# A hybrid decoder layer on Trainium2: TensorE in written order through the mixer, the recurrence woven with projection pieces, and the modulation sums taken by rows

## The chip, the cores and the metric

The kernel runs on one core of a Trainium2 chip. The metric is the device time of one execution in microseconds (us). The engines are named as the profile names them: PE is TensorE (matmuls; PEld its weight loads), DVE is VectorE, ACT is ScalarE, POOL is GpSimd, SP is SyncE, which issues most loads. Each engine carries out its own instruction list in order; semaphores tie the lists together.

## The reference, cut to what matters

One layer over 2048 tokens of width 1024, float32, batch 1. The part that the change touches is the mixer:

```python
cond = silu(c)
mod = cond @ ada_w + ada_b              # six vectors of 1024: shift, scale, gate, twice
h = rms_norm(x, mix_norm_g) * (1 + scale_m) + shift_m
q_a, k_a, v_a, q_h, f_h, i_h, g_h = split(h @ w_in + b_in)
attn = rms_norm(sliding_window_gqa_with_sinks(q_a, k_a, v_a, sinks))    # window 128, 8 heads of 64
rec  = hgrn2(silu(q_h), lb + (1 - lb) * sigmoid(f_h), i_h)              # 4 heads of 128
#      f_t = forget gate; S_t = diag(f_t) S_{t-1} + (1 - f_t) i_t^T ; o_t = S_t^T q_t
rec  = rms_norm(rec) * silu(g_h)                                        # output gate
x = x + gate_m * (concat(attn, rec) @ w_out)
```

Behind it stand a second norm with its own modulation, a gated MLP with a causal convolution, and a final norm. These are not touched.

## The kernel before, in words

Every float32 product is made of three matmuls on parts rounded to a high and a low piece (`mm3`: high by high, high by low, low by high). A projection of 128 columns over 512 tokens is 24 matmuls of 128x512 into one bank of PSUM. Its weights arrive as a raw tile, ACT rounds the high piece, and DVE or POOL subtracts to get the low one (`split`), a projection or two ahead of use (`weights`, in the order of the list `units`).

The mixer runs from about 88 to 930 us, as a loop over four groups `g` of 512 tokens. In a group the projections are named by what they give: `hq`, `hf` (query and forget gate of a recurrent head), `i` (two halves of 192 matmuls of 128x256 each), `k`, `q` (tiles `ps_q`, weights `w_qp`), `v`, and `hg` (output gate of a head; tile `ps_hg`). The recurrence is worked in two pairs of heads, (0,1) and (2,3). For a pair:

- The preparation, on DVE with rounding on ACT and POOL: products `raw0` to `raw2` of query and key, running products `tot` of the forget gate, and in-place scalings of the query `a_q` and the key `K` by `tot`.
- Five levels of widths 4, 8, 16, 32, 64. A level group (`lv`) is four matmuls of one head; in between DVE scales `a_q` and `K` for the next level (`scaled`) and copies the result under a mask into `AT` (ACT does so for 32 and 64). After them three sums per head (`lv_d`, `lv` from `ph`, `pl`, `p` by `ones_r`), with four masked copies of DVE behind them, and a transpose of `K` (`ktp`).
- `hg_state`: the state update (`U`, `mid`) and the output `ho`.

Level groups, sums and `ktp` share two PSUM banks (tag `hg`); projections have three (tag `mm`). A scheduling layer orders each engine's list by the dependences that it sees and program order as priority, except where `pin` holds an engine to the order written. Before the change only ACT (`S`) is pinned, and only from place to place; PE's order is the scheduler's.

The modulation vectors of later layers are made piece by piece beside this (`after`, six places in a group): each piece is a 512 KB load of 128 columns of `ada_w` on SP's queue, then on DVE one product 128x1024 and sums of 512, 256 and 128 columns (tiles `ada`, `part`). There are 24 of them. The attention of a group is 16 units of score, softmax and value work (tiles `sc`, `comb`, `st`, `pT`, `att_o`), with the four output gates (`hg_out`: a projection, four transposes `otp`, and one DVE product into `a_g`) written behind it.

Of the kernel before, what the change touches and what calls it, by code (L numbers as in the profile page):

```python
# [8 lines left out]
F32 = mybir.dt.float32  # L9
# [9 lines left out]
P = 128  # L19
# [34 lines left out]
def kernel(ctx, tc, x, c, ada_w, ada_b, mix_norm_g, w_in, b_in, attn_sinks, attn_out_g,  # L54
# [152 lines left out]
    def mod_part(t, raw, to):  # L207

        SY.dma_start(out=raw, in_=ada_v[:, :, t * P:(t + 1) * P])
        V.tensor_tensor(out=raw, in0=raw, in1=cond.unsqueeze(2).broadcast_to([P, KT, P]), op=ALU.mult)  # L210
        for n in (4, 2):
            V.tensor_tensor(out=raw[:, 0:n, :], in0=raw[:, 0:n, :], in1=raw[:, n:2 * n, :], op=ALU.add)
        V.tensor_tensor(out=to[:, t % 4, :], in0=raw[:, 0, :], in1=raw[:, 1, :], op=ALU.add)

# [15 lines left out]
    with ExitStack() as mx:  # L230
# [103 lines left out]
        for g in range(NG):  # L334
# [6 lines left out]
            add(("i", 0), load_wi, 0)  # L341
            add(("i", 1), load_wi, 1)
# [4 lines left out]
            add(("k", 0), load_w, 512)  # L347
            add(("qp", 0), load_wq, 0)
            add(("qp", 1), load_wq, 1)
            add(("v", 0), load_w, 640)  # L350
            for h in range(4):
                add(("hg", h), load_w, 2304 + h * P)
# [223 lines left out]
        defer = list(range(16, 40))  # L576

        part = []

        def mod_cols():  # L580
            if part:
                mod_cols_of(*part.pop())
# [6 lines left out]
        for g in range(NG):  # L589
            hhi, hlo = hh  # L590

            def after():

                if defer:
                    t = defer.pop(0)
                    if t % 4 == 0:
                        mod_cols()
                        part.append((t, mt2.tile([P, 4, P], F32, tag="part", bufs=1, name=f"part_{t}")))
                    mod_part(t, mt2.tile([P, KT, P], F32, tag="ada", bufs=1, name=f"ada_{t}"), part[-1][1])

# [6 lines left out]
            def proj_i():  # L607
                i_tok = mt.tile([P, BPG, 512], F32, tag="i_tok", bufs=1, name=f"itok_{g}")
                for pp in range(2):
                    ws = weights(g, "i", pp)  # L610
                    for bp in range(2):
                        ps = bank(f"ps_i{g}_{pp}_{bp}", "mm").rearrange("p (a b) -> p a b", a=2)
                        for bb in range(2):
                            b = 2 * bp + bb
# [9 lines left out]
            def proj_attn():  # L624
# [37 lines left out]
                for b in range(BPG):  # L662
                    TE.transpose(ps[:, b * P:(b + 1) * P], vT[:, b * P:(b + 1) * P], ident)
# [921 lines left out]
```

## Time and profile before

| | us |
|---|---|
| median of three runs | 2443.85 (2443.26 to 2449.54) |
| the profiled execution, whole | 2448.34 |
| its span in the profile | 2446.3 |
| of it, the mixer's recurrence stretches (four) | 579.30 |
| of it, the mixer's attention stretches (four) | 263.10 |
| granted clock, mean | 0.975 |

The four recurrence stretches are 88 to 210.3, 274 to 426, 489 to 640 and 707 to 861 us of the span: from a group's first projections to the end of the second pair. The four attention stretches are what lies between them and up to 930. The rest of the span, before 88 and behind 930, is set-up and the MLP. The granted clock is the mean share of TensorE's full clock; a stretch at half of it reads 0.50.

### The profile page before, as it was taken

The page shows a single profiled execution, that of the slowest core. Times are in us where ns is not written, and L with a number is a line of the kernel's source. Part 1 is how long each engine was busy: PE and PEld are TensorE (multiplying, and loading weights), DVE is VectorE, ACT ScalarE, POOL GpSimd, SP SyncE. Part 2 cuts the span into 40 slices and gives each one's busy share as a digit, 9 for nine tenths or more (in the row PEclk, how much of TensorE's full clock was granted, in tenths as well). Part 3 has the DMA queues.
Part 4 walks back from the last instruction along what each step waited for, and adds up shares of the span by engine and source line. Part 5 has one row for each costly group of instructions (what it writes and reads, how often), then busy time and mean ns, then how long its engine had stood idle before and what let it go on. Part 6 is the DMA issues. An engine that isn't in the chain of part 4 may idle for free. (4 is left out here: it accounts for less than half of the span.)

```text
span 2446.3 us, 31473 instructions
## 1 busy us (share of the span) xinstructions
PE 2294.8 (94%) x11521; PEld 1904.1 (78%) x11521; DVE 1912.5 (78%) x2737; ACT 966.7 (40%) x1658; POOL 931.7 (38%) x776
## 2 busy tenths in 40 slices
PE   5889898998999899999999999999999989998997
PEld 4877787887788787887888888778888768786775
DVE  8888768788867877378888888878878688777666
ACT  3336523723552363455333333433333343233322
POOL 6222212213122222032756666478888721110101
PEclk8999999999999999999999999999999989999999
DMA  8342323323231238475434433554555488887543
GB/s 216 91 121 91 91 69 105 95 70 112 79 95 53 86 113 267 157 248 155 146 97 144 151 117 114 191 176 156 163 153 166 138 267 248 215 209 239 182 171 124
DMA packets 335445, 359.74 MB, mean 147 GB/s; under 512 B 12405, under 2 KB 279371, under 8 KB 335291
## 3 DMA queue, kind: packets, MB, share of 16 engines
q1 hardware_dynamic: 320315, 301.36, 39.3%
q0 software_dynamic: 14976, 56.37, 8.5%
q8 instruction: 91, 1.49, 0.2%
q14 instruction: 63, 0.52, 0.1%
HBM read 250.19 MB, written 107.49 MB: 146 GB/s over the span
## 5 line engine op out<-in xcount | busy, mean ns | idle before, releaser
L46 DVE SCALAR_TENSOR_TENSOR cc<-ub,cols,cc 128x1024 f32<-128x1024 f32 x88 | 153.2, 1741 | 15.5 <-ACT cc L46 13.3
L46 PE MATMUL lv<-a_q,K 128*128 128x128 f32 (+2 forms) x768 | 80.5, 265 | 42.7 <-DVE K L46 38.2
L46 ACT ACTIVATE Th<-da 128x896 fp32r<-128x896 f32 x88 | 81.8, 945 | 92.6 <-PE ps_d L46 88.2
L46 PEld LDWEIGHTS lv<-a_q,K 128*128 128x128 f32 (+2 forms) x768 | 72.2, 177 | 55.6 <-DVE K L46 28.8
L46 POOL DMA_DIRECT2D x_d<-o x32 | 27.2, 858 | 218.6 <-DVE o L46 218.6
L46 DVE TENSOR_TENSOR o<-ps_d,u 128x512 f32<-128x512 f32 x72 | 49.5, 687 | 71.6 <-ACT u L46 34.8
L46 DVE TENSOR_TENSOR Tl<-da,Th 128x896 fp32r<-128x896 f32 x88 | 94.5, 1099 | 12.8 <-ACT Th L46 12.8
L46 POOL TENSOR_TENSOR s<-wu_0r,s 128x512 f32<-128x512 f32 x44 | 59.2, 1347 | 107.2 <-DVE ws_0l L46 14.6
L46 DVE TENSOR_TENSOR cc<-cc,v 128x1024 f32<-128x1024 f32 x44 | 64.2, 1459 | 43.5 <-ACT cc L46 43.4
L46 POOL MEMSET AT<- 128x512 f32 x16 | 8.5, 533 | 234.8 <-PE ho L46 211.8
L46 POOL TENSOR_TENSOR s<-wu_1r 128x512 f32<-128x512 f32 x44 | 70.0, 1590 | 70.7 <-DVE t_T4l L46 16.2
L46 POOL TENSOR_TENSOR wu_1r<-wu_0r,wu_1r 128x512 f32<-128x512 f32 x44 | 93.3, 2121 | 3.1
L46 ACT ACTIVATE cc<-cc 128x1024 f32<-128x1024 f32 x44 | 46.7, 1061 | 120.8 <-DVE cc L46 120.8
L46 POOL TENSOR_SCALAR rv_d<-ssd 128x1 f32<-128x1 f32 x16 | 14.8, 925 | 181.6 <-ACT dx L46 181.6
L46 POOL TENSOR_TENSOR pl<-raw,ph 128x512 fp32r<-128x512 f32 x32 | 44.3, 1388 | 99.3 <-ACT ph L46 83.6
L46 POOL TENSOR_TENSOR s<-s,wu_0r 128x512 f32<-128x512 f32 x44 | 73.6, 1672 | 0.0
L46 DVE TENSOR_TENSOR v<-ps_u,v 128x512 f32<-128x512 f32 x88 | 60.4, 686 | 15.2 <-PE ps_u L46 11.9
L46 DVE COPY_PREDICATED AT<-lev,lv 128x512 f32<-128x512 uint32 (+1 forms) x96 | 70.1, 731 | 2.4 <-PE lv L46 1.1
L46 ACT ACTIVATE cc<-ub,cols 128x1024 f32<-128x1024 f32 x44 | 54.6, 1240 | 25.9 <-DVE ub L46 25.9
L46 DVE TENSOR_TENSOR ada<-ada,cond 128x1024 f32<-128x1024 f32 (+1 forms) x37 | 52.3, 1414 | 14.3 <-DMA ada<-in_ada_w_dram 14.3
L46 DVE TENSOR_TENSOR a_q<-a_q,tot 128x256 f32<-128x256 f32 x96 | 52.1, 543 | 12.4 <-PE lv L46 11.1
L46 DVE TENSOR_TENSOR ada<-ada 128x512 f32<-128x512 f32 (+3 forms) x82 | 61.2, 747 | 0.9
(2114 smaller groups left out, 8562.9 us busy)
## 6 DMA issues: line engine op xcount, KB each, us to landing
da<-act_d SPq DMA_DIRECT2D x88, 448.0 KB, 8.0
wu_0r<-in_w_up_dram SPq DMA_DIRECT2D x44, 512.0 KB, 4.6
wu_1r<-in_w_up_dram SPq DMA_DIRECT2D x44, 512.0 KB, 4.3
act_d<-cc POOLq DMA_DIRECT2D x42, 512.0 KB, 4.1
ada<-in_ada_w_dram SPq DMA_DIRECT2D x40, 512.0 KB, 6.0
x_d<-o POOLq DMA_DIRECT2D x32, 512.0 KB, 7.9
act_d<-sm POOLq DMA_DIRECT2D x21, 768.0 KB, 4.2
x<-in_x_dram SPq DMA_DIRECT2D x26, 512.0 KB, 5.6
```

The lines of the kernel that those rows point to most:

```text
L46: ins = fn(*args, **kwargs)
```

## The change

It does four things.

1. PE is pinned with ACT to written order from a group's first projection to the end of its second pair. Projections become generators that yield after each six matmuls (`steps`; `steps_i` after each twelve), and `weave` takes one such piece behind each level group, each sum and each transpose of a pair.
2. The pieces: the second half of `i` and the next `hq` go into the first pair's levels, the next `hf` into its state; `q` 2 and 3 and the output gates of heads 0 and 1 into the second pair's levels, `v` into its state. `k` moves ahead of the first pair. The weights' list follows.
3. The preparation of a head becomes a function of its own (`hg_prep`) and stands behind that head's `hf`, with other projections between it and the pair's first level.
4. The modulation sums go by rows: 48 steps, each a 256 KB load of 2 KB rows and one DVE product-and-sum 128x512, one step ahead in its load; one step before and one behind the second pair's levels, ten in each attention.

```diff
-    def mod_part(t, raw, to):
-        SY.dma_start(out=raw, in_=ada_v[:, :, t * P:(t + 1) * P])
-        V.tensor_tensor(out=raw, in0=raw, in1=cond.unsqueeze(2).broadcast_to([P, KT, P]), op=ALU.mult)
...
+        def load_mod():
...
+                raw = mt2.tile([P, 4 * P], F32, tag="ada", bufs=2, name=f"ada_{n}_{k}")
+                SY.dma_start(out=raw, in_=ada_v[:, k, 16 * P + n * 4 * P:16 * P + (n + 1) * 4 * P])
+        def mod_step():
...
+            if k == 0:
+                V.tensor_scalar(out=acc_, in0=raw, scalar1=cond[:, 0:1], scalar2=None, op0=ALU.mult)
+            else:
+                V.scalar_tensor_tensor(out=acc_, in0=raw, scalar=cond[:, k:k + 1], in1=acc_, op0=ALU.mult, op1=ALU.add)
...
+            def steps(w, name, fn):
+
+                w, ps = w(), bank(name, "mm")
+                for k in range(KT):
+                    mm3(ps, w[0][:, k, :], w[1][:, k, :], hhi[:, k, :], hlo[:, k, :], k == 0, k == KT - 1)
+                    if k % 2 and k < KT - 1:
+                        yield
+                fn(ps)
+                yield
...
+            def weave(gen, *fill):
+
+                rest = (i for one in fill for i in one)
+                next(rest, None)
+                for _ in gen:
+                    next(rest, None)
+                for _ in rest:
+                    pass
...
                     values(u)
+                    for _ in range(2 if u % 4 == 3 else 1):
+                        mod_step()
...
-                for h in range(2):
-                    proj_h(hg_q, h, "hq")
-                    proj_h(hg_f, h, "hf")
-            weights(g, "i", 0, ahead=1)
-            pin(True, S)
-            hg_scores((0, 1))
-            i_tok = proj_i()
-            hg_state((0, 1))
...
+                run(steps_h(hg_q, 0, "hq"), steps_h(hg_f, 0, "hf"), steps_h(hg_q, 1, "hq"))
+                hg_prep(0)
+                run(steps_h(hg_f, 1, "hf"))
+            hg_prep(1)
+            run(steps_i(0), steps(lambda: weights(g, "k", 0), f"ps_k{g}", take_k))
+            q2 = [] if g == 0 else [steps_h(hg_q, 2, "hq")]
+            weave(hg_scores((0, 1)), steps_i(1), *q2)
+            weave(hg_state((0, 1)), steps_h(hg_f, 2, "hf"))
+            hg_prep(2)
+            mod_step()
+            run(steps_h(hg_q, 3, "hq"), steps_h(hg_f, 3, "hf"))
+            hg_prep(3)
+            run(steps_q(0), steps_q(1))
+            weave(hg_scores((2, 3)), steps_q(2), steps_q(3), steps_h(hg_out, 0, "hg"), steps_h(hg_out, 1, "hg"))
+            mod_step()
+            weave(hg_state((2, 3)), steps(lambda: weights(g, "v", 0), f"ps_v{g}", take_v))
+            pin(False, S, TE)
+            v_tok = turn_v()
```

Three places show what this does to the engines' lists. All are of group 1 and its second pair; in the names the first number is the group, the second the head, a third the level, and the last a running number of the buffer.

On DVE, before, while head 3 is prepared (`ada_26` is a modulation piece, `kl` the key's low piece, `w1_qp` weights of `q`):

```order
L46 TENSOR_TENSOR ada_26_3707<-ada_26_3707,cond_157 128x1024
L46 SCALAR_TENSOR_TENSOR kl0_705<-ps_k1_3713,cols_137,kd0_703 64x512
L46 TENSOR_TENSOR ada_26_3707<-ada_26_3707 128x512
L46 SCALAR_TENSOR_TENSOR kl1_706<-ps_k1_3713,cols_137,kd1_704 64x512
L46 TENSOR_TENSOR ada_26_3707<-ada_26_3707 128x256
L46 TENSOR_TENSOR part_24_3353<-ada_26_3707 128x128
L46 TENSOR_TENSOR w1_qp_1_1l_3417<-w1_qp_1_0r_3418,w1_qp_1_1h_3416 128x512
L46 TENSOR_TENSOR w1_qp_1_1l_3417<-w1_qp_1_1r_3425,w1_qp_1_1h_3416 128x512
L46 TENSOR_TENSOR raw1_1_3_3460<-a_q1_3_3342,K_1_3_3406 128x256
L46 TENSOR_TENSOR raw2_1_2_3468<-a_q1_2_3258,K_1_2_3303 128x512
L46 TENSOR_TENSOR a_q1_3_3342<-a_q1_3_3342,f_1_3_3403 128x256
L46 TENSOR_TENSOR K_1_3_3406<-K_1_3_3406,f_1_3_3403 128x256
```

and DVE there now:

```order
L46 TENSOR_TENSOR w1_qp_1_0l_3422<-w1_qp_1_0r_3425,w1_qp_1_0h_3421 128x512
L46 TENSOR_TENSOR w1_qp_1_1l_3424<-w1_qp_1_0r_3425,w1_qp_1_1h_3423 128x512
L46 TENSOR_TENSOR w1_qp_1_0l_3422<-w1_qp_1_1r_3432,w1_qp_1_0h_3421 128x512
L46 TENSOR_TENSOR w1_qp_1_1l_3424<-w1_qp_1_1r_3432,w1_qp_1_1h_3423 128x512
L46 TENSOR_SCALAR f_1_3_3464<-f_1_3_3464,omc_614,lbc_612 128x512
L46 TENSOR_SCALAR K_1_3_3467<-f_1_3_3464 128x512
L46 TENSOR_TENSOR tot_1_3_1_3487<-f_1_3_3464 128x256
L46 TENSOR_TENSOR raw0_1_3_3476<-a_q1_3_3416,K_1_3_3467 128x512
L46 TENSOR_TENSOR tot_1_3_2_3495<-tot_1_3_1_3487 128x128
L46 TENSOR_TENSOR a_q1_3_3416<-a_q1_3_3416,f_1_3_3464 128x512
L46 TENSOR_TENSOR tot_1_3_4_3601<-tot_1_3_2_3495 128x64
L46 TENSOR_TENSOR raw1_1_3_3481<-a_q1_3_3416,K_1_3_3467 128x256
```

The modulation piece and the key's pieces have left the preparation; what stands in it now is the weights of `q`, ahead of it, and the head's own work.

On PE, before, where the second pair's levels begin (`lv_1_2_4` is group 1, head 2, level 4):

```order
L46 MATMUL ps_q1_1_3785<-hlo_1_2521,w1_qp_0_1h_3362 128x512
L46 MATMUL lv_1_2_4_3488<-a_q1_2_3258,K_1_2_3303 128x128 x4
L46 MATMUL lv_1_3_4_3498<-a_q1_3_3342,K_1_3_3406 128x128 x4
L46 MATMUL ps_q1_1_3785<-hhi_1_2520,w1_qp_0_1l_3363 128x512
L46 MATMUL ps_q1_2_3822<-hhi_1_2520,w1_qp_1_0h_3414 128x512
L46 MATMUL ps_q1_2_3822<-hlo_1_2521,w1_qp_1_0h_3414 128x512
L46 MATMUL ps_q1_2_3822<-hhi_1_2520,w1_qp_1_0l_3415 128x512
L46 MATMUL lv_1_2_8_3508<-a_q1_2_3258,K_1_2_3303 128x128 x4
L46 MATMUL ps_q1_2_3822<-hhi_1_2520,w1_qp_1_0h_3414 128x512
L46 MATMUL lv_1_3_8_3518<-a_q1_3_3342,K_1_3_3406 128x128 x4
L46 MATMUL ps_q1_2_3822<-hlo_1_2521,w1_qp_1_0h_3414 128x512
L46 MATMUL ps_q1_2_3822<-hhi_1_2520,w1_qp_1_0l_3415 128x512
```

and PE there now:

```order
L46 MATMUL ps_q1_2_3571<-hhi_1_2522,w1_qp_1_0l_3422 128x512
L46 MATMUL lv_1_2_4_3578<-a_q1_2_3207,K_1_2_3322 128x128 x4
L46 MATMUL ps_q1_2_3571<-hhi_1_2522,w1_qp_1_0h_3421 128x512
L46 MATMUL ps_q1_2_3571<-hlo_1_2523,w1_qp_1_0h_3421 128x512
L46 MATMUL ps_q1_2_3571<-hhi_1_2522,w1_qp_1_0l_3422 128x512
L46 MATMUL ps_q1_2_3571<-hhi_1_2522,w1_qp_1_0h_3421 128x512
L46 MATMUL ps_q1_2_3571<-hlo_1_2523,w1_qp_1_0h_3421 128x512
L46 MATMUL ps_q1_2_3571<-hhi_1_2522,w1_qp_1_0l_3422 128x512
L46 MATMUL lv_1_3_4_3594<-a_q1_3_3416,K_1_3_3467 128x128 x4
L46 MATMUL ps_q1_2_3571<-hhi_1_2522,w1_qp_1_0h_3421 128x512
```

The first level group used to stand in the middle of `ps_q1_1`, with one to three projection matmuls behind each of the next; it now comes behind `ps_q1_0`, `ps_q1_1` and six matmuls of `ps_q1_2`, and six follow each level group.

On DVE, before, from the first level group on (`a_q` and `K` by `tot_1_2_2` are the scaling of head 2 that its level 8 needs):

```order
L46 TENSOR_TENSOR a_q1_2_3258<-a_q1_2_3258,tot_1_2_2_3482 128x64x4
L46 TENSOR_TENSOR K_1_2_3303<-K_1_2_3303,tot_1_2_2_3482 128x64x4
L46 COPY_PREDICATED AT_1_2_3432<-lev4_680,lv_1_2_4_3488 128x512
L46 TENSOR_TENSOR a_q1_3_3342<-a_q1_3_3342,tot_1_3_2_3486 128x64x4
L46 TENSOR_TENSOR K_1_3_3406<-K_1_3_3406,tot_1_3_2_3486 128x64x4
L46 COPY_PREDICATED AT_1_3_3433<-lev4_680,lv_1_3_4_3498 128x512
L46 TENSOR_TENSOR a_q1_2_3258<-a_q1_2_3258,tot_1_2_4_3495 128x32x8
L46 TENSOR_TENSOR K_1_2_3303<-K_1_2_3303,tot_1_2_4_3495 128x32x8
L46 COPY_PREDICATED AT_1_2_3432<-lev8_685,lv_1_2_8_3508 128x512
L46 TENSOR_TENSOR a_q1_3_3342<-a_q1_3_3342,tot_1_3_4_3505 128x32x8
L46 TENSOR_TENSOR K_1_3_3406<-K_1_3_3406,tot_1_3_4_3505 128x32x8
L46 COPY_PREDICATED AT_1_3_3433<-lev8_685,lv_1_3_8_3518 128x512
```

and DVE there now:

```order
L46 TENSOR_TENSOR a_q1_2_3207<-a_q1_2_3207,tot_1_2_2_3368 128x64x4
L46 TENSOR_TENSOR K_1_2_3322<-K_1_2_3322,tot_1_2_2_3368 128x64x4
L46 COPY_PREDICATED AT_1_2_3342<-lev4_680,lv_1_2_4_3578 128x512
L46 TENSOR_TENSOR w1_hg_0l_3500<-w1_hg_0r_3497,w1_hg_0h_3499 128x1024
L46 SCALAR_TENSOR_TENSOR q_1_00_3528<-ps_q1_0_3503,cols_137,q_1_00_3528 64x512
L46 SCALAR_TENSOR_TENSOR q_1_01_3529<-ps_q1_0_3503,cols_137,q_1_01_3529 64x512
L46 SCALAR_TENSOR_TENSOR q_1_10_3559<-ps_q1_1_3534,cols_137,q_1_10_3559 64x512
L46 SCALAR_TENSOR_TENSOR q_1_11_3560<-ps_q1_1_3534,cols_137,q_1_11_3560 64x512
L46 TENSOR_TENSOR a_q1_3_3416<-a_q1_3_3416,tot_1_3_2_3495 128x64x4
L46 TENSOR_TENSOR K_1_3_3467<-K_1_3_3467,tot_1_3_2_3495 128x64x4
L46 COPY_PREDICATED AT_1_3_3469<-lev4_680,lv_1_3_4_3594 128x512
L46 TENSOR_TENSOR a_q1_2_3207<-a_q1_2_3207,tot_1_2_4_3585 128x32x8
```

The two evictions of each of `ps_q1_0` and `ps_q1_1` and the low piece of the output gate's weights now stand between the first level's masked copy and the scaling of head 3 for level 8.

## Rows read from the trace of the kernel before

**Rows 1.** The page: busy time, share of the span and instructions of each engine.

```profile
PE 2294.8 (94%) x11521; PEld 1904.1 (78%) x11521; DVE 1912.5 (78%) x2737; ACT 966.7 (40%) x1658; POOL 931.7 (38%) x776
```

**Rows 2.** Waits of PE, mixer: total us, times, longest us.

```profile
PE lv L46 <- DVE K L46: 38.2, 7, 7.0
PE lv L46 <- DVE AT L46: 5.5, 6, 1.9
PE ps_i L46 <- DVE w_i_1l L46: 4.6, 1, 4.6
...
PE U L46 <- DVE AT L46: 2.8, 4, 0.8
```

**Rows 3.** Windows over the four recurrence stretches: stretch, us, busy us by engine, clock.

```profile
core 0: us, PE busy (x) PEld busy (x) DVE busy (x) ACT busy (x) POOL busy (x), PEclk, DMA share, GB/s
88.00:210.30 122.30, 106.84 (x693) 91.27 (x692) 110.86 (x214) 37.33 (x64) 29.52 (x28) 0.96 0.30 87
...
707.00:861.00 154.00, 141.14 (x870) 121.57 (x868) 120.95 (x222) 53.21 (x85) 36.42 (x29) 0.96 0.24 69
sum 579.30, PE 525.87 PEld 452.23 DVE 479.31 ACT 190.57 POOL 133.74; mean PE 131.47 PEld 113.06 DVE 119.83 ACT 47.64 POOL 33.44
```

**Rows 4.** Windows over the four attention stretches, same columns.

```profile
210.30:274.20 63.90, 57.84 (x380) 50.48 (x379) 53.67 (x129) 49.31 (x135) 18.93 (x22) 0.97 0.36 107
...
861.00:930.00 69.00, 64.01 (x405) 54.92 (x404) 48.54 (x107) 43.41 (x121) 19.54 (x17) 1.00 0.39 129
sum 263.10, PE 244.47 PEld 213.22 DVE 202.90 ACT 190.59 POOL 73.51; mean PE 61.12 PEld 53.30 DVE 50.72 ACT 47.65 POOL 18.38
```

**Rows 5.** Timeline of PE at group 1's second pair: start, duration, operation, wait.

```profile
381.49 0.39 PE L46 MATMUL ps_q<-hhi,w_qp_1h 128*128 128x512 f32 x1
381.72 0.39 PE L46 MATMUL ps_q<-hlo,w_qp_1h 128*128 128x512 f32 x1
389.14 3.75 PE L46 MATMUL lv<-a_q,K 128*128 128x128 f32 x16 [7.04 <-DVE K L46]
```

**Rows 6.** Windows over such a stall and what follows, and over another's end.

```profile
384.00:389.10 5.10, 0.00 (x0) 0.00 (x0) 5.10 (x9) 2.13 (x4) 2.40 (x2) 0.51 0.98 263
389.10:392.50 3.40, 3.35 (x16) 3.38 (x17) 2.59 (x6) 1.17 (x2) 1.40 (x1) 0.50 0.28 69
392.50:394.40 1.90, 1.90 (x7) 1.54 (x7) 1.54 (x4) 1.03 (x2) 0.94 (x1) 0.52 0.00 0
100.00:104.50 4.50, 4.12 (x22) 4.12 (x23) 4.48 (x11) 1.68 (x3) 3.31 (x2) 0.62 0.80 225
```

**Rows 7.** Timeline of DVE ahead of that stall.

```profile
367.39 1.23 DVE L46 TENSOR_TENSOR ada<-ada,cond 128x1024 f32<-128x1024 f32 x1 [3.78 <-DMA ada<-in_ada_w_dram]
...
377.95 1.23 DVE L46 TENSOR_TENSOR ada<-ada,cond 128x1024 f32<-128x1024 f32 x1 [1.47 <-DMA ada<-in_ada_w_dram]
...
387.99 0.68 DVE L46 TENSOR_TENSOR raw<-a_q,K 128x512 f32<-128x512 f32 x1
```

**Rows 8.** Groups of DVE by shape, mixer: total busy us, mean ns, idle before.

```profile
L46 DVE TENSOR_TENSOR a_q<-a_q,tot 128x256 f32<-128x256 f32 x96 | 52.1, 543 | 12.4 <-PE lv L46 11.1
...
L46 DVE TENSOR_TENSOR K<-K,tot 128x256 f32<-128x256 f32 x96 | 42.1, 439 | 0.0
...
L46 DVE COPY_PREDICATED AT<-lev,lv 128x512 f32<-128x512 uint32 x48 | 35.0, 730 | 0.0
...
L46 DVE TENSOR_TENSOR raw<-a_q,K 128x512 f32<-128x512 f32 x32 | 29.5, 921 | 0.0
L46 DVE TENSOR_TENSOR ada<-ada,cond 128x1024 f32<-128x1024 f32 x23 | 29.4, 1279 | 12.2 <-DMA ada<-in_ada_w_dram 12.2
...
L46 DVE SCALAR_TENSOR_TENSOR q<-ps_q,cols,q 64x512 fp32r<-64x512 f32 x32 | 24.0, 750 | 1.0
...
L46 DVE SCALAR_TENSOR_TENSOR a_g<-otp,cols,a_g 128x512 f32<-128x512 f32 x16 | 11.9, 742 | 2.8 <-POOL a_g L46 2.7
...
L46 DVE TENSOR_TENSOR w_i_0l<-w_i_0r,w_i_0h 128x1024 fp32r<-128x1024 f32 x6 | 7.4, 1226 | 15.7 <-ACT w_i_0h L46 13.9 <-DMA ada<-in_ada_w_dram 1.7
```

**Rows 9.** Windows over the four attention stretches, modulation tiles on DVE alone.

```profile
sum 263.10, DVE 13.09; mean DVE 3.27
```

More of the change, by code (lines that the diff above doesn't have):

```diff
@@ L605, in proj @@
                 return ps
[L607 to L614, printed above, removed]
-                            bs = slice(b * P, (b + 1) * P)
-                            for k in range(KT):
-                                wh, wl = (t[:, k % 4, :] for t in ws[k // 4])
-                                mm3(ps[:, bb, :], hhi[:, k, bs], hlo[:, k, bs], wh, wl, k == 0, k == KT - 1)
-                        cs = slice(pp * 256, (pp + 1) * 256)
-                        V.tensor_tensor(out=i_tok[:, 2 * bp:2 * bp + 2, cs], in0=ps,
-                                        in1=bi_bc[:, cs].unsqueeze(1).broadcast_to([P, 2, 256]), op=ALU.add)
-                return i_tok
@@ L624, in proj_attn, with steps_i @@
-            def proj_attn():
-                ps = proj(weights(g, "k", 0), f"ps_k{g}")
+            def steps(w, name, fn):
[6 more added lines that the diff above has]
+                yield
+            def steps_i(pp):
+                ws = weights(g, "i", pp)
+                for bp in range(2):
+                    ps = bank(f"ps_i{g}_{pp}_{bp}", "mm").rearrange("p (a b) -> p a b", a=2)
+                    for bb in range(2):
+                        b = 2 * bp + bb
+                        bs = slice(b * P, (b + 1) * P)
+                        for k in range(KT):
+                            wh, wl = (t[:, k % 4, :] for t in ws[k // 4])
+                            mm3(ps[:, bb, :], hhi[:, k, bs], hlo[:, k, bs], wh, wl, k == 0, k == KT - 1)
+                            if k == 3 or k == KT - 1 and bb == 0:
+                                yield
+                    cs = slice(pp * 256, (pp + 1) * 256)
+                    V.tensor_tensor(out=i_tok[:, 2 * bp:2 * bp + 2, cs], in0=ps,
+                                    in1=bi_bc[:, cs].unsqueeze(1).broadcast_to([P, 2, 256]), op=ALU.add)
+                    yield
@@ L658, in proj_attn, with take_q @@
-                ps = proj(weights(g, "v", 0), f"ps_v{g}")
+            qT, vts = [], []
+            def take_q(ps):
+                j = len(qT)
+                pair = [qa.tile([P, GT], F32R, tag=f"q{j}{e}", name=f"q_{g}_{j}{e}") for e in range(2)]
+                for e in range(2):
+                    hp = slice(e * 64, e * 64 + 64)
+                    S.activation(pair[e][hp, :], ps[hp, :], AF.Identity, bias=col("qb", j)[hp, :])
+                for e in range(2):
+                    hp = slice(e * 64, e * 64 + 64)
+                    op = slice(64 - e * 64, 128 - e * 64)
+                    V.scalar_tensor_tensor(out=pair[e][op, :], in0=ps[hp, :], scalar=col("qb", j)[hp, :],
+                                           in1=pair[e][hp, :].bitcast(F32), op0=ALU.add, op1=ALU.subtract)
+                qT.append(pair)
@@ L781, in hg_scores @@
             def hg_scores(hs_):
-                for h in hs_:
-                    ats[h] = mt.tile([P, 4, P], F32, tag="AT", name=f"AT_{g}_{h}")
-                    tots[h] = fs[h]
                 def full(h, label):
@@ L969 @@
                 tb = late.enter_context(tc.tile_pool(name="tb", bufs=1, side="right", reuse_waits="tile"))
[L970 to L974 removed]
+            weights(g, "hg", 2)
+            attention(qT, v_tok)
             for h in range(4):
```

194 lines of the change are left out of this document (92 added, 102 removed).

## The prediction

> **What bounds the kernel now.** I read the page first, then the windows, then the waits. On the page PE is busy for 94% of the span [rows 1]; the reader is to see that there is little idle time to win anywhere, so that a gain has to be idle time of PE or a slow clock that goes away. The windows say where these lie. In the four recurrence stretches PE is busy for 525.9 of 579.3 us and DVE for 479.3 [rows 3]: 53 us without PE. In the four attention stretches PE is busy for 244.5 of 263.1 and DVE for 202.9 [rows 4]: 19 us. So PE sets the pace in both, with DVE close behind it in the recurrence.
>
> The waits name the 53 us. PE's level groups wait 38.2 us in seven waits for DVE's `K`, and one matmul of `i` waits 4.6 us for a low piece of its weights [rows 2]: with it one stall of 4 to 7 us for each of the eight pairs, where the scheduler has run out of projections before the preparation is done. The timeline shows one: PE goes from a projection matmul each 0.23 us into 7.04 us of nothing [rows 5]. DVE is busy ahead of it with two modulation pieces that also wait 3.78 and 1.47 us for their own loads [rows 7]. Behind the stall the granted clock is half: 0.51 in it, then 0.50 and 0.52 for 5.3 us of work, so 2.6 us are lost after the wait; behind a shorter one the clock reads 0.62 over 4.5 us, which is 3.4 us at half and 1.7 lost [rows 6].
>
> **The change part by part.** All sums are against the profiled execution, 2448.34 us; the median of the runs is 4.5 lower, and I carry the sum over to 2443.85.
>
> *What goes.* (1) The eight stalls, 38.2 + 4.6 = 42.8 us [rows 2]. A head's preparation now starts behind its own forget gate, and between the last one and the first level stand two projections of `q` (48 x 0.23 = 11 us) or half of `i` and `k`. Head 3's work on DVE, from its gate to the first level, is three products at 0.92, four scalings by pairs at 0.98 and some short ones [rows 8], some 9 us, and the modulation pieces are out of it. I take all of it; the bound is that half comes back (a rival). (2) The clock behind the stalls, eight times the mean of 2.6 and 1.7: 17 us [rows 6]. (3) The short waits inside the old weaving, `lv` and `U` for `AT`, 5.5 + 2.8 = 8.3 us [rows 2], which I count anew under (5). Together -68.
>
> *What is moved in.* (4) Eight output gates go from the attention into the second pairs. Each is 24 matmuls of 0.23 us [rows 5], 5.5 us, and four transposes, 0.5 us at half that pitch each: 8 x 6.0 = +48 us of PE in the recurrence.
>
> *What waits now.* (5) PE may no longer take another matmul when DVE is late, so DVE's list has to be followed by hand. In the second pair, from the first level group to head 3's level 8, PE has three groups and 18 pieces: a group is 0.84 us at full clock (two took 3.4 us at half [rows 6]), 3 x 0.84 + 18 x 0.23 = 6.7 us. DVE has behind the first group (0.84) a scaling pair 0.98, a masked copy 0.73, the low piece of a weight tile 1.23, four `q` evictions at 0.75, a scaling pair and the copy that frees the PSUM bank, 0.98 + 0.73 [rows 8]: 8.5 us. That is 1.8 us of waiting, and I add 0.9 for the next weight piece and evictions; 4 x 2.7 = 11. In the first pair's sums the pieces run out. DVE makes its first copy, idles until the second sum at 2.1 us (0.46 + six pieces), then seven copies of 0.73 end at 7.2, while PE would want the bank at 4.1: 3.1 us, four times 12. For low pieces of weights that DVE makes behind a preparation I have only the one wait of 4.6 [rows 2]; between nothing and eight such waits, 37 us, I take 12, since each weight is asked for one or two projections ahead and that wait was in the first group. Together +35; the bounds are +10 and +60.
>
> The recurrence stretches then take 579 - 68 + 48 + 35 = 594 us.
>
> *The attention.* (6) It loses 48 us of PE work (196 of 244 stay), and PE no longer bounds it. DVE has 202.9 us now [rows 4]; 13.1 of modulation pieces go [rows 9], eight gate products go with their projections at 0.74 [rows 8], 5.9, and 40 row steps come. The trace has no such step. The nearest row is the `q` eviction, the same kind of instruction over 512 columns, 0.75 us; the dearest is the product of two tiles of the same shape, 0.92 [rows 8]. I take 0.75: 40 x 0.75 = 30. So DVE needs 202.9 - 13.1 - 5.9 + 30 = 214 us. The largest share that DVE reaches in any stretch is 110.9 of 122.3, 0.91 [rows 3]; the largest in an attention is 53.7 of 63.9, 0.84, with PE as the bound [rows 4]. At 0.91 the attention takes 235 us, -28; at 0.84 it takes 255, -8; I take -28, because now DVE is the engine with the most to do, as it was in the stretch with 0.91.
>
> The remaining eight row steps lie in the recurrence (6 us of DVE beside PE's projections); if that cover were gone they cost these 6. `k` and the split `hg_prep` move at nothing while projections of 11 us hide them. The loads of the row steps are half as large and twice as many, with the same bytes; the core's DMA engines are busy for 0.24 to 0.39 of these stretches [rows 3, 4].
>
> A row step also reads two tiles of SBUF. Rows of that kind stretch here: the product `raw` takes 0.68 us alone [rows 7] and 0.92 in the mean, while a masked copy, with one input from PSUM, keeps 0.73 [rows 8]. The Trainium skill (SBUF — State Buffer, "Who interferes with whom") has a rule for it: a DVE instruction with two SBUF inputs contends with a GpSimd instruction that reads SBUF. By that rule, the trace agrees, the steps belong at the dearer price, and the sum would be 40 x 0.17 = 7 us higher; it stands below as a rival.
>
> **Sum**: -68 + 48 + 35 - 28 = -13 us.
>
> **The rivals.** *The weaving covers everything.* Waits under (5) halve (-17), and DVE reaches 0.96 in the attention (223 us, -12 more): 2443.9 - 13 - 29 = 2402 us. For it: six matmuls (1.4 us) behind each level group are nearly the masked copy and scaling (1.7 us). Against it: no stretch shows a share of 0.96.
>
> *Written order makes every level wait (slower).* Before, the scheduler put one to three matmuls where they fitted; now each of the 80 level groups needs DVE's copy of two groups ago, and any stretch of DVE's list goes to PE undamped. At 0.5 us each it is 40 us: 2471. It decides from (13 + 7.3) / 80 = 0.25 us a group. For it: DVE works through most of the recurrence already, 479 of 579 us [rows 3], and copy plus scaling are longer than the piece. Against it: PE's waits there outside the stalls are 8.3 us now [rows 2].
>
> *The attention does not shrink.* The row steps stand in DVE's list between softmax steps, and a step whose load is late holds the softmax. Twenty-three pieces waited 12.2 us for theirs [rows 8], 0.53 each; 40 x 0.53 = 21 us: 2452. For it: only one load is ahead. Against it: each is half as large.
>
> *POOL holds the row steps*: +7, 2438 us.
>
> *It does not do what it says.* The first levels still wait half as long, since DVE makes weight pieces ahead of the preparation: half of 43 + 17 is 30: 2461 us.
>
> **How the numbers follow.** A measurement of this kernel can tell about 0.3%, 7.3 us: faster is below 2436.5, slower above 2451.2. The forecast, 2443.9 - 13 = 2431, has a chance of 0.42, with a range of its own of 2418 to 2444 (faster 0.32, same 0.10). Everything covered, 0.22, faster. Every level waits, 0.14: slower 0.12, same 0.02. The attention does not shrink, 0.13: same 0.06, slower 0.07. POOL, 0.05: same. Not what it says, 0.04: slower. That makes faster 0.54, same 0.23, slower 0.23. Both signs hold much, so the range goes from a little below the covered case to a little below the slow one, 2394 to 2464, with about 0.08 left out below and 0.11 above.
>
> **What would show it.** In the changed kernel's waits, `lv` for `K` should be down from 38.2 us to a few; if there is one wait of 3 us or more left for each pair, step (1) is wrong. The recurrence stretches should come to 594 us with a granted clock of 0.98 or more, and the four attentions to 235. If `lv` waits for `AT` in dozens of short waits, the slow rival holds; if DVE's `part` steps wait for their loads by over 10 us, the attention rival does. The prediction is wrong as a whole if the recurrence takes over 615 us, or the attention over 255.

## The result, and the profile after

The changed kernel takes 2476.21 us (median of four runs, 2474.18 to 2478.61) against 2444.68 for the kernel before beside it: a ratio of 1.0121, with a 95% interval of 1.0105 to 1.0137. It is 1.2% slower, where 2431 was forecast; the range ended at 2464. The profiled execution has a span of 2472.4 us at a granted clock of 0.971.

On the page PE's share stays at 94% (compare [rows 1]), of a longer span:

```profile
PE 2315.5 (94%) x11521; PEld 1914.2 (77%) x11521; DVE 1897.2 (77%) x2689; ACT 961.5 (39%) x1653; POOL 921.5 (37%) x776
```

The waits of PE in the mixer, which now ends near 960 us (columns as in [rows 2]; `osb` and `pc` are tiles of the attention):

```profile
PE lv L46 <- DVE AT L46: 17.3, 9, 3.2
PE att_t L46 <- DVE osb L46: 13.1, 7, 2.8
PE att_o L46 <- DVE pc L46: 9.9, 16, 1.2
PE ktp L46 <- DVE AT L46: 8.6, 8, 1.2
PE ps_i L46 <- ACT w_i_0h L46: 8.0, 1, 8.0
...
PE lv L46 <- DVE K L46: 1.8, 2, 1.0
```

The reader is to see that the wait named in the prediction is gone: `lv` for `K`, 38.2 us in [rows 2], is 1.8. In its place `lv` waits for `AT` for 17.3 us, `ktp` for `AT` for 8.6, one matmul of `i` for ACT for 8.0, and in the attention `att_t` and `att_o` wait for 13.1 and 9.9 (4.2 and 1.8 before, by the same view).

For the windows the groups are cut anew in both kernels, at the first matmul of a group's `hq` and at its first score; the last attention ends at 930 us before and at 960 now. The recurrence before, the sum by this cut, and then two groups and the sum after:

```profile
sum 593.90, PE 540.52 PEld 463.92 DVE 489.07 ACT 197.19 POOL 131.99; mean PE 135.13 PEld 115.98 DVE 122.27 ACT 49.30 POOL 33.00
```

```profile
88.00:228.20 140.20, 120.78 (x746) 102.38 (x745) 108.38 (x195) 46.62 (x77) 34.01 (x29) 0.94 0.25 76
...
510.30:667.80 157.50, 149.93 (x919) 127.23 (x917) 120.06 (x207) 58.09 (x91) 35.97 (x31) 0.99 0.27 79
...
sum 616.60, PE 574.26 PEld 487.45 DVE 465.08 ACT 219.76 POOL 140.62; mean PE 143.57 PEld 121.86 DVE 116.27 ACT 54.94 POOL 35.16
```

The attention, group 1 and the sum before, and then all four after:

```profile
427.00:482.00 55.00, 54.15 (x374) 48.24 (x372) 43.38 (x115) 44.47 (x133) 16.98 (x22) 1.00 0.31 92
...
sum 248.10, PE 229.41 PEld 201.13 DVE 192.74 ACT 183.61 POOL 75.26; mean PE 57.35 PEld 50.28 DVE 48.18 ACT 45.90 POOL 18.81
```

```profile
228.20:286.40 58.20, 52.05 (x321) 45.43 (x321) 47.63 (x124) 38.52 (x124) 12.93 (x22) 0.85 0.32 104
445.90:510.30 64.40, 53.48 (x346) 45.91 (x345) 51.63 (x137) 39.90 (x128) 13.44 (x22) 0.89 0.37 119
667.80:731.10 63.30, 53.34 (x338) 46.12 (x337) 48.27 (x130) 39.79 (x128) 13.65 (x22) 0.87 0.29 96
890.50:960.00 69.50, 62.48 (x373) 54.42 (x372) 55.19 (x122) 41.87 (x117) 17.66 (x16) 0.90 0.52 163
sum 255.40, PE 221.36 PEld 191.88 DVE 202.72 ACT 160.08 POOL 57.67; mean PE 55.34 PEld 47.97 DVE 50.68 ACT 40.02 POOL 14.42
```

The recurrence has grown by 22.7 us, 593.9 to 616.6, of which 17.9 lie in the first group (122.3 to 140.2). The attention has grown by 7.3, 248.1 to 255.4, although 48 us of PE's work have left it. Of this, 3.4 us lie between a group's first score and its last value product (220.3 to 223.7 for the four), 11.3 between that product and the next group's first `hq`, and the stretch behind the last value product is 7.4 shorter. The column behind the last bracket, the granted clock, reads 0.85 to 0.90 where it read 0.97 to 1.00 [rows 4]; at that clock PE is busy for 221.4 us, where 229.4 less the 48 that were moved out would be 181. The remaining -4 us of the span lie behind the mixer.

Cut finer, group 1's attention after shows when that comes about:

```profile
445.90:470.00 24.10, 22.62 (x142) 19.20 (x142) 20.04 (x55) 18.36 (x58) 7.94 (x13) 1.00 0.47 154
470.00:490.00 20.00, 15.93 (x124) 13.98 (x123) 18.07 (x53) 16.39 (x57) 4.04 (x5) 1.00 0.25 79
490.00:500.00 10.00, 7.80 (x48) 6.80 (x48) 7.93 (x20) 1.73 (x9) 0.73 (x2) 0.74 0.32 102
500.00:506.00 6.00, 3.16 (x15) 3.00 (x15) 2.35 (x7) 0.72 (x2) 0.73 (x2) 0.50 0.30 94
```

The two output gates that are left fill PE to about 468 us. Behind them PE is busy for 15.9 of 20 us, still at full clock; from 495 us on the clock is half, and the attention's small matmuls, which wait for DVE (`att_t` and `att_o` above), run at that.

### The profile page after: what moved, and what is told of

It is laid out like the page before. It is cut to its first block, busy times and chain, and to the rows that moved or that the text cites. A ratio compares the mean times of both kernels' runs of the same rounds, so it can differ in the third digit from the quotient of the medians.

```text
span 2472.4 us, 31410 instructions
## 1 busy us (share of the span) xinstructions
PE 2315.5 (94%) x11521; PEld 1914.2 (77%) x11521; DVE 1897.2 (77%) x2689; ACT 961.5 (39%) x1653; POOL 921.5 (37%) x776
## 5 line engine op out<-in xcount | busy, mean ns | idle before, releaser
L46 POOL DMA_DIRECT2D x_d<-o x32 | 27.2, 858 | 217.1 <-DVE o L46 216.9
L46 PEld LDWEIGHTS lv<-a_q,K 128*128 128x128 f32 (+2 forms) x768 | 65.1, 161 | 31.0 <-issue 27.7
L46 POOL TENSOR_TENSOR a_q<-a_q,s_q 128x512 f32<-128x512 f32 x16 | 23.7, 1482 | 174.2 <-ACT s_q L46 174.2
L46 PE MATMUL lv<-a_q,K 128*128 128x128 f32 (+2 forms) x768 | 72.9, 249 | 16.0 <-DVE AT L46 12.8
L46 DVE TENSOR_TENSOR v<-ps_u,v 128x512 f32<-128x512 f32 x88 | 60.3, 686 | 14.7 <-PE ps_u L46 11.3
L46 DVE TENSOR_TENSOR a_q<-a_q,tot 128x256 f32<-128x256 f32 x96 | 43.7, 456 | 25.6 <-PE lv L46 25.2
L46 PE MATMUL att_o<-vtok,pc 128*128 128x64 f32 x256 | 53.5, 298 | 9.9 <-DVE pc L46 9.9
L46 DVE TENSOR_TENSOR ot<-ps_o,gate 128x512 f32<-128x512 f32 x32 | 22.0, 687 | 50.5 <-PE ps_o L46 50.5
```

The source lines that it names most:

```text
L46: ins = fn(*args, **kwargs)
```

## The experiments

Fourteen kernels were run, each beside the kernel before; since its median moved between 2444.7 and 2451.0 from one set of runs to the next, ratios are compared. Theory A is: the attention lost the work that filled PE and kept up its clock. Theory B was the rival from the prediction: row steps hold the softmax in DVE's list. Later a second pair of theories was needed, on the written order of PE.

**The gates back.**

```diff
...
-            weave(hg_scores((2, 3)), steps_q(2), steps_q(3), steps_h(hg_out, 0, "hg"), steps_h(hg_out, 1, "hg"))
+            weave(hg_scores((2, 3)), steps_q(2), steps_q(3))
...
-                if h > 1:
-                    run(steps_h(hg_out, h, "hg"))
+                run(steps_h(hg_out, h, "hg"))
```

The list of weights follows, where the first `...` stands.

> The changed kernel with the output gates of heads 0 and 1 back behind the attention; all else as changed. Theory A (the attention lost its filler: with two gates instead of four PE runs out of projections half way, its chain of softmax steps shows and the clock falls): the four attention stretches stay near 255 us although 24 us of gates per pair of groups, 48 in all, come back, with a granted clock of 0.95 or more against 0.85 to 0.90; the recurrence stretches lose 48 and gain some 10 of waits where the second pair has no pieces: about 2440 us. Theory B (the row steps in DVE's list hold the softmax): the attention gets the 48 us on top, about 300, and the kernel stays at 2475 to 2490.

Measured: 1.0043 (1.0026 to 1.0060), 2459 us where A had 2440. The four attentions are below, cut as above but the last one at its last value product, first the change's own sum, then group 1 and the sum of this kernel:

```profile
sum 247.60, PE 213.56 PEld 185.50 DVE 199.57 ACT 159.35 POOL 56.65; mean PE 53.39 PEld 46.38 DVE 49.89 ACT 39.84 POOL 14.16
```

```profile
440.10:505.70 65.60, 61.07 (x403) 53.52 (x401) 56.57 (x139) 48.52 (x137) 18.41 (x25) 0.95 0.46 138
...
sum 242.50, PE 229.00 PEld 201.82 DVE 204.89 ACT 180.29 POOL 67.90; mean PE 57.25 PEld 50.46 DVE 51.22 ACT 45.07 POOL 16.97
```

With 48 us more work for PE the attention is 5 us shorter, at a clock of 0.95 to 1.00. That is A, and it speaks against B. But the recurrence came down by 21 us, not 38, to 595.5, 1.6 more than before the change: something in it costs as much as the old stalls did.

**No row steps.**

```diff
         def mod_step():
+            return
```

> The changed kernel without the 48 row steps and their loads (the modulation of the later layers is left out and a constant stands in its place). Theory A: the attention stays between 245 and 255 us with a clock under 0.92, and the kernel at 2462 to 2474. Theory B: the attention falls to 225 to 235 us and the kernel to about 2450.

This kernel leaves the later layers' modulation out. Measured: 1.0074 (1.0052 to 1.0096). Group 1's attention and the sum:

```profile
442.20:503.80 61.60, 53.60 (x330) 47.68 (x329) 44.49 (x117) 39.92 (x128) 12.12 (x22) 0.83 0.20 65
...
sum 246.80, PE 214.37 PEld 187.86 DVE 178.72 ACT 159.24 POOL 53.22; mean PE 53.59 PEld 46.97 DVE 44.68 ACT 39.81 POOL 13.31
```

Without any row step, and with 21 us less on DVE, the attention takes 246.8 us against 247.6, with the clock lower still at 0.83 in this group. B falls. The kernel as a whole is 3.9 us shorter in the profiles (2468.5 against 2472.4) and 0.5% by the ratios; where that lies outside the attention stays open.

**The first group's weights early.**

```diff
                 hg_q(2, ps0[4])
+                weights(0, "k", 0, ahead=1)
```

> The changed kernel with the weights of the second half of i asked for ahead of head 1's preparation in the first group, so that ACT rounds them before that head's pieces. If the 18 us that the first recurrence stretch grew by come from the wait of 8.0 us for ACT and what follows it, that wait goes and the kernel takes 2464 to 2468; if the preparation itself is late, the wait moves to the first level and it stays within 3 us of 2476.

Measured: 1.0098 (1.0076 to 1.0120), whose interval overlaps that of the change. The 8.0 us wait for ACT went, and the waits of the first recurrence stretch now read:

```profile
PE lv L46 <- DVE K L46: 6.3, 3, 4.5
...
PE ps_i L46 <- DVE w_i_0l L46: 2.5, 1, 2.5
```

The preparation itself is late there: the wait moved to the first level, and the stretch takes 138.1 us against 140.2. The first group has no projections ahead of its preparation, since set-up has made them.

**Rows alone.** The kernel before, with `mod_step` in the change's places in place of `after`, and no other part of the change.

> The kernel before with the modulation by row steps alone, in the places where the change has them; PE is ordered by the scheduler and all four gates stay behind the attention. Theory A: four gates cover the steps, the attention grows by no more than 5 us with a clock of 0.95 or more, and the preparations are freed of the old pieces, so that the stalls of 42.8 us shrink: 2425 to 2445. Theory B: the attention grows by 15 us or more: 2450 to 2460.

Measured: 0.9975 (0.9966 to 0.9984), slightly faster. The recurrence:

```profile
sum 569.80, PE 528.15 PEld 453.51 DVE 450.91 ACT 193.85 POOL 127.95; mean PE 132.04 PEld 113.38 DVE 112.73 ACT 48.46 POOL 31.99
```

It falls by 24 us, as A had it, and the attention to the last value product grows by 16, from 232.9 (248.1 less what lies behind 914.8 us) to 249.0, as B had it; both theories had one half right here. Part of both is the cut itself, since PE's scheduler may place a group's first `hq` freely: it stands later behind the last value product, by 11.0 us for three groups (12.6 to 23.6), and that lengthens the attention and shortens the recurrence. From first score to last value product the attention takes 225.4 us against 220.3, so in this order of PE the steps there cost it 5 us, and two of its four stretches read a clock of 0.90 and 0.92.

**Useless work in the attention.**

```diff
                     run(steps_h(hg_out, h, "hg"))
+                    run(steps(lambda: weights(g, "hg", h), f"ps_x{g}_{h}", lambda ps: S.activation(
+                        mt2.tile([P, 2], F32, tag="xjunk", bufs=1, name=f"xj{g}_{h}"), ps[:, 0:2], AF.Copy)))
```

> The changed kernel with two more projections in each attention, whose results nobody uses (44 us of TensorE work in all). Theory A (the attention lacks TensorE work to keep the clock up, and its chain runs at half clock): the work is free, the attention stretches go from 247.6 to 235 to 245 us with a clock of 0.95 or more, and the kernel stays at 2464 to 2478. Rival (the chain over DVE and ACT sets the attention, the clock only follows): the attention grows by 15 to 44 us, and the kernel takes 2490 to 2520.

Measured: 1.0127 (1.0106 to 1.0149) against 1.0121. The first two groups' attentions and the sum:

```profile
226.30:284.10 57.80, 54.60 (x368) 47.79 (x368) 46.95 (x123) 37.17 (x125) 13.03 (x22) 1.00 0.32 105
444.70:506.80 62.10, 58.69 (x394) 51.58 (x393) 50.42 (x135) 40.58 (x130) 13.25 (x22) 0.97 0.37 112
...
sum 239.10, PE 225.34 PEld 198.46 DVE 194.10 ACT 156.78 POOL 50.72; mean PE 56.34 PEld 49.62 DVE 48.53 ACT 39.20 POOL 12.68
```

The attentions are 8.5 us shorter than the change's 247.6 with more for PE to do, and the clock is back at 0.95 to 1.00. Nearly all 192 useless matmuls run inside them, between the first score and the last value product. What that gains is given back behind the last attention: from the last value product to the first matmul of the MLP it takes 197.8 us against 188.5. In the change the first 26 matmuls of the output projection had run ahead of that product; here 5 do, and the useless ones run there. This is the plainest reading of A: 44 us of matmuls for nothing. It also bounds the clock's part: with a clock near 1 the attention still takes 239 us, no less than the 232.9 that it took before with all four gates in it.

**PE free.** Only the pin of PE is taken out; all code stands where the change has it.

```diff
-            pin(True, S, TE)
+            pin(True, S)
...
-            pin(False, S, TE)
+            pin(False, S)
```

> The changed kernel, with PE left to the scheduler in the recurrence as before (ACT stays in written order). If the written order of PE costs time in the recurrence (with the gates back it still took 595.5 us against 569.8 of the rows alone), the recurrence falls by 15 us or more and the kernel to 2450 to 2462; if only the moved gates cost it, it stays within 5 us of 2476.

Measured: 0.9952 (0.9936 to 0.9968), faster than the kernel before. This was the surprise of the study: 1.7% of the time for two words. From the first half of `i` to the first score (in the first group, from 88 us), group 1 and the sum, with PE in written order and then free:

```profile
308.30:445.90 137.60, 130.56 (x822) 111.34 (x820) 101.10 (x176) 45.95 (x74) 31.55 (x28) 0.96 0.25 72
...
sum 549.50, PE 507.90 PEld 433.16 DVE 411.50 ACT 183.41 POOL 127.17; mean PE 126.98 PEld 108.29 DVE 102.87 ACT 45.85 POOL 31.79
```

```profile
88.00:219.00 131.00, 117.71 (x743) 99.03 (x742) 108.06 (x193) 46.39 (x77) 34.83 (x29) 0.96 0.27 81
296.10:426.50 130.40, 126.36 (x821) 107.50 (x820) 101.02 (x177) 45.92 (x74) 32.16 (x29) 1.00 0.27 77
...
sum 522.30, PE 496.90 PEld 421.52 DVE 412.07 ACT 183.80 POOL 129.76; mean PE 124.22 PEld 105.38 DVE 103.02 ACT 45.95 POOL 32.44
```

Written order takes 27.2 us more in these stretches. The timeline shows one place of it. In written order, in group 1's second pair:

```profile
401.38 0.39 PE L46 MATMUL ps_q<-hlo,w_qp_0h 128*128 128x512 f32 x1
401.61 0.40 PE L46 MATMUL ps_q<-hhi,w_qp_0l 128*128 128x512 f32 x1
405.20 1.36 PE L46 MATMUL lv<-a_q,K 128*128 128x128 f32 x8 [3.20 <-DVE AT L46]
406.21 0.77 PE L46 MATMUL ps_q<-hhi,w_qp_1h 128*128 128x512 f32 x1
406.79 0.63 PE L46 MATMUL ps_q<-hlo,w_qp_1h 128*128 128x512 f32 x1
```

and free:

```profile
386.62 0.40 PE L46 MATMUL ps_q<-hhi,w_qp_1h 128*128 128x512 f32 x1
386.85 0.40 PE L46 MATMUL ps_q<-hlo,w_qp_1h 128*128 128x512 f32 x1
389.00 1.13 PE L46 MATMUL lv<-a_q,K 128*128 128x128 f32 x8 [1.75 <-DVE AT L46]
389.89 0.48 PE L46 MATMUL ps_q<-hhi,w_qp_1l 128*128 128x512 f32 x1
```

Third level group done, the written order has six matmuls, and then head 3's level 8 waits 3.20 us for the bank that DVE frees behind four `q` evictions. The next matmuls take 0.77 and 0.63 us each: the clock has halved. The granted clock over the wait, and over what follows:

```profile
401.80:405.20 3.40, 0.20 (x1) 0.03 (x1) 3.31 (x7) 2.42 (x3) 0.00 (x0) 1.00 0.49 142
406.20:409.90 3.70, 3.70 (x15) 3.12 (x15) 3.59 (x8) 0.00 (x0) 0.00 (x0) 0.57 0.49 142
```

So it is in all four groups: waits of 3.20 to 3.22 us, and 0.77 and 0.63 behind them. The scheduler puts eleven matmuls there (five of the next `ps_q`), the wait is 1.75 us, and the matmul behind it takes 0.48. The clock of group 1's whole window is 0.96 against 1.00.

**The rows in the recurrence.** Two runs place all twelve row steps of a group there: one from the rows alone, one from the kernel with the gates back in written order.

> The kernel before with row steps, all twelve of a group in its recurrence and none in the attention; PE by the scheduler, gates behind the attention. Rows alone with ten steps in the attention took 569.8 us of recurrence and 249.0 of attention (to the last value product), the kernel before 593.9 and 232.9. If the steps cost the attention by their place in DVE's list there, the attention goes back to 233 to 238, the recurrence to 572 to 580, and the kernel to 2425 to 2435; if not, it stays near 2445.

> The changed kernel with the gates back behind the attention and the row steps in the recurrence: of the change, the written order and the rows are left. If the written order costs the recurrence 20 to 25 us against the scheduler, it takes 590 to 600 us there, 233 to 238 in the attention, and 2446 to 2456 in all; if it costs nothing, it goes with the kernel of the rows in the recurrence, 2425 to 2435.

Measured: 1.0004 (0.9992 to 1.0015) and 1.0167 (1.0142 to 1.0192). The attention of the first did return, to 237.3 us by the cut above (223.4 from first score to last value product, against 225.4), but its recurrence grew:

```profile
sum 586.30, PE 541.04 PEld 464.43 DVE 476.51 ACT 195.72 POOL 131.59; mean PE 135.26 PEld 116.11 DVE 119.13 ACT 48.93 POOL 32.90
```

586.3 against 569.8 us: the steps cost more in the recurrence than they did in the attention, 0.29% of the kernel by the ratios (0.9975 to 1.0004). Both expectations were wrong on the recurrence and on the kernel. In the second kernel the recurrence went from 595.5 with the gates back to 617.6: there moving the steps costs 1.24% (1.0043 to 1.0167), four times as much. The two pairs of kernels differ in the written order of PE, and in the early preparation and the order of the code too.

**Which part of the written order.** PE held from the first half of `i` on, and the reverse:

```diff
-            pin(True, S, TE)
+            pin(True, S)
...
             hg_prep(1)
+            pin(True, TE)
             run(steps_i(0), steps(lambda: weights(g, "k", 0), f"ps_k{g}", take_k))
```

> The changed kernel with PE held to written order only from the first half of i on; the first projections of a group are the scheduler's, as in the run with PE free (2437, against 2476 of the change). Read from the traces of those two, the stretches from the first half of i to the first score differ by 27 us in the four groups, those from the first score to the next group's i by 12. If the written order costs at the groups' seams, this kernel gets those 12 back: 2460 to 2467; if it costs mostly there, 2437 to 2450.

> The reverse: PE held to written order for a group's first projections only, and free from the first half of i on. If the weaving by hand is what costs, this gets the 27 us: 2444 to 2455; if the seams are, 2465 to 2475.

Measured: 1.0088 (1.0071 to 1.0106) and 0.9997 (0.9988 to 1.0007). Against the change's 1.0121 the first projections, at the seams between groups, give back 0.3% (8 us) and the woven part 1.2% (30 us), where 12 and 27 us had been read from the two traces.

**PE free and the gates back**, and the early weights with PE free:

> The change with PE free and the output gates of heads 0 and 1 back behind the attention. With PE free and the gates in the recurrence the kernel took 2437. If moving the gates costs by itself (the attention lost its filler), 2425 to 2433; if a free PE places them well either way, 2434 to 2442; if they pay in the recurrence, 2445 or more.

> The change with PE free and, in the first group, the weights of the second half of i rounded ahead of head 1's preparation. With PE free one wait of 7.8 us for that rounding is left in the first group. If the projections can then fill it, 2427 to 2433; if the preparation is late anyway, within 4 us of 2437.

Measured: 0.9891 (0.9876 to 0.9906), 2421.6 us, and 0.9946 (0.9927 to 0.9965). The early weights give nothing that can be told from 0.9952. The gates back give 15 us (0.9952 to 0.9891), more than expected: even a free PE loses by the move. From the first `i` to the first score (the first group from 88 us), group 1 and the sum:

```profile
292.80:414.40 121.60, 116.33 (x772) 98.84 (x770) 96.14 (x176) 41.80 (x68) 28.95 (x26) 1.00 0.24 71
...
sum 488.70, PE 457.73 PEld 387.52 DVE 393.18 ACT 167.48 POOL 117.66; mean PE 114.43 PEld 96.88 DVE 98.30 ACT 41.87 POOL 29.41
```

The recurrence is 33.6 us shorter than with the gates in it (522.3), and from a group's first score to the next group's first `i`, or in the last group to the MLP, the kernel is 14.6 us longer.

**Two pieces at the one place.** The written order again, with twelve matmuls behind the third level group of the second pair:

```diff
-                for _ in gen:
+                for n, _ in enumerate(gen):
                     next(rest, None)
+                    if n in twice:
+                        next(rest, None)
...
+                  twice=(2,))
```

> The changed kernel, PE in written order, with two pieces in place of one behind the third level group of the second pair, where PE waited 3.20 us and its clock fell; the pieces behind it move up by one. With PE free the scheduler puts eleven matmuls there. If that one place is most of what the written order costs in the levels, four times the wait of 3.2 us and of the clock behind it come back, less what the missing piece costs at the end: 2462 to 2468. If the cost is spread over all levels and the sums, it stays at 2472 to 2480.

Measured: 1.0066 (1.0049 to 1.0083). The waits of `lv` for `AT` in the mixer:

```profile
PE lv L46 <- DVE AT L46: 12.8, 13, 1.5
```

The longest wait is 1.5 us in place of 3.2, and 0.55% (13 us) of the 1.2% come back: that one place, four times, is nearly half of what the weaving cost. The rest was not taken apart; no wait of `lv` for `AT` is over 1.5 us any more.

**All that helped.**

> PE free, gates behind the attention, and the weights of the first group's second half of i rounded early: the three edits that each gave something. With PE free, and gates back it took 2421.6; the early rounding gave 2 of 2437 there. 2417 to 2422 if they add up.

Measured: 0.9881 (0.9862 to 0.9899), not to be told from 0.9891. The version to keep is PE free with the gates back.

## Why the prediction was wrong, point by point

The runs leave out one part of the change at a time, so each part of the sum has a measurement, here in us of the 2445 by the ratios. The attention is cut in every kernel at a group's first score and last value product, which stay where they are when PE's order changes; the sums over the four groups are, of one profiled execution each:

| kernel | 88 us, or last value product, to first score | first score to last value product | behind the last one |
|---|---|---|---|
| before | 606.5 | 220.3 | 1531.5 |
| the change | 640.5 | 223.7 | 1520.2 |
| gates back | 621.0 | 217.0 | 1529.0 |
| no row steps | 638.8 | 223.0 | 1518.7 |
| useless work | 641.2 | 215.3 | 1533.4 |
| PE free | 606.6 | 217.6 | 1522.8 |
| PE free, gates back | 573.4 | 218.6 | 1534.1 |

**Two steps failed. The first is (1) to (3)**, the stalls, the clock behind them and the old short waits: "I take all of it", -68. The kernel with PE free and the gates back has this part of the change and the rows, and neither written order nor moved gates. It gains 27 us (0.9891), and rows by themselves give 6 of these (0.9975). The stalls did go: `lv` for `K` fell from 38.2 us to 1.8 in the change and to 1.0 here. But the time did not come back with them. From 88 us to the last value product, before and in this kernel:

```profile
88.00:914.80 826.80, 756.35 (x4789) 654.08 (x4788) 672.22 (x1357) 373.84 (x829) 199.56 (x194) 0.96 0.30 89
```

```profile
88.00:880.00 792.00, 749.03 (x4799) 637.88 (x4799) 651.82 (x1307) 380.34 (x836) 194.43 (x194) 0.98 0.30 90
```

PE's idle time falls from 70.5 to 43.0 us, by 27.5 where (1) and (3) have 51, and its busy time by 7.3 where the clock of (2) has 17: 34.8 us, about half. Other waits are there now, one of 7.8 us for the weights of `i` in the first group, which gained nothing up to its first score (122.3 to 123.9), 8.9 of `lv` and 3.6 of `ktp` for `AT`. Even with (3) left out of the forecast, since a free PE may keep those waits, it is 27 for 60. In the sum this is the larger miss, 33 to 41 us, about the 39 by which the span was missed (2446.3 - 13 forecast, 2472.4 measured). Why the other half stays away is open.

**The second is (6)**, the attention: "I take -28, because now DVE is the engine with the most to do". The work was counted well. A row step takes 0.767 us, where 0.75 was taken and 0.92 was the rival's price:

```profile
L46 DVE SCALAR_TENSOR_TENSOR part<-ada,cond,part 128x512 f32<-128x512 f32 x41 | 31.5, 767 | 0.1
```

All but one of them take 0.72 to 0.75, and one takes 1.81. The rival's 0.92 was such a mean too: of the 32 products `raw`, 28 took 0.68 to 0.69 and four 1.8 to 2.9. DVE is busy for 202.7 us in the four stretches of the result. But it reached a share of 0.79, not 0.91: DVE's work does not set the attention. With the gates out and the row steps in, the stretches were 7 us longer; without the row steps' 21 us on DVE they stayed as they were; with 44 us of useless work for PE they were 8 shorter. By the table, first score to last value product takes 215 to 224 us in all of these kernels, with two gates in it or four. The gates had been filler there, and taking them out freed 1 us with PE free, and lost 6.7 in written order, where the clock fell. What else came back lies behind the last value product, 11.3 us and 8.8. In all that is -12 and -2 where -28 was forecast.

**Step (4)**, the gates at +48 in the recurrence, was too dear, and that hid (6). The eight gates' matmuls and transposes are busy for 55.7 us there, but moving them lengthened the time ahead of the scores by 33.2 us with PE free and by 19.5 in written order. So (4) and (6) together, +20 in the sum, came to 15 and 19 us (0.9952 to 0.9891, 1.0121 to 1.0043): right in total, by two errors that cancel, which is luck.

**Step (5)**, the waits in written order, +35, was right in size: 41 us with the gates moved (1.0121 less 0.9952), 37 with them back (1.0043 less 0.9891). The place was named too, level 8 of head 3 behind the `q` evictions, with 3.2 us there for the 1.8 worked out. Not named were the clock behind that wait and the 8 us at the seams. The parts add up: -27 + 37 + 19 = +29, and 1.0121 is +30.

By the windows alone one would read it otherwise: recurrence +22.7 where +15 was forecast (-68 + 48 + 35), attention +7 for -28. There the missing gain of (1) to (3) hides behind the gates: with these back the recurrence is 1.6 us longer than before where -33 (-68 + 35) was forecast, and moving them in adds 21.1 where 48 was. Of the prediction's signs, the attention's came true: 255 meant 8 less than before, and it took 7 more.

**The rivals.** "Written order makes every level wait" was near in time, 2471 us, but by luck: its 40 us come on top of the 35 of (5), and the written order cost 37 to 41 in all. Nor was it 80 waits of half a us: a 3.2 us wait with its clock in each group gave 13 us, the seams between groups 8. "It does not do what it says" had the size, half of the stalls' price, but its condition, first levels that still wait for `K`, is not met. "The attention does not shrink" was right in effect and wrong in cause: no row step waited for its load (0.1 us in all, the group above), and without them it was as long. That POOL holds the row steps did not show: 0.767 us in the mean for its 0.92.

So the change in its parts, by ratios: rows by themselves -0.25%; rows, early preparation and the new order of the code, PE free, -1.1%; written order of PE +1.5 to 1.7%; gates moved +0.6 to 0.8%.

What stays open is what sets the 215 us and more from first scores to last value products at a clock near 1: its chain of score, mask, exponent, transpose and value through three engines was not taken apart. Open too is which part of the free version's 1.1% comes from the early preparation and which from the order of the code, since they were not run apart.

## What to carry to other kernels

Work of the busiest engine that fills another stage's waits can cost next to nothing there, and moving it out then gains next to nothing: here 1 us in the attention, for 33 in the recurrence. Before moving it, ask which waits it fills, and whether the clock would fall without it. An engine that is 93% busy in a stage need not be what sets the stage; ask what the stage's chain of dependences takes when the filler is gone.

A wait that disappears from a view is not yet time gained: 38.2 us of stalls went to 1.0, and with the clock behind them and all else 27 us came back. Leave out one part of a change at a time and set each term of the sum against that; a sum by stages can hide one wrong term behind another.

A hand-written order fixes how much work stands behind each wait, and one lump on another engine's list (here four evictions and a weight piece) cost 13 of the 30 us that the woven part lost; a scheduler's order with the same code let eleven matmuls stand where six were not enough. Changes that come as one are worth running apart: here the rows, the early preparation and the new order of the code gave 1.1%, and the written order and the moved gates took 2.3%.

## What the runs showed of the hardware that was not expected

Adding 44 us of matmuls to the attention changed the kernel's time by less than its measurement is uncertain (1.0127 against 1.0121), and made the attention itself 8.5 us shorter: its granted clock rose from 0.85 to 0.90 up to 0.95 to 1.00. One level down, the granted clock read 1.00 over a wait of 3.20 us behind full work and 0.57 over the 3.7 us that followed, where the projection matmuls took 0.77 and 0.63 us after 0.39 and 0.40 ahead of it; behind a wait of 1.75 us in the same place the next took 0.48, and the window read 1.00. The length of the wait alone does not decide it: in the change's last attention, at 898.5 us and also behind full work, the clock read 0.61 over the 2.7 us behind a wait of 1.76, and projection matmuls took 0.78.

Of the 42 row steps of the form shown above, which read two tiles of SBUF, 41 took 0.72 to 0.75 us and one 1.81; of the 32 products `raw` before, 28 took 0.68 to 0.69 and four 1.8 to 2.9. The products' mean of 0.92 is the price of none of them.
